# Attention's small products two pairs of heads at a time, in five spots of a layer in place of six

## The chip, the cores and the metric

One core of a Trainium2 chip runs the whole program. The metric is the device time of one launch in microseconds (us). The engines are TensorE (PE, matrix products; PEld is its loading of the stationary operand), VectorE (DVE, elementwise work and reductions), ScalarE (ACT, activations and copies), GpSimd (POOL) and SyncE (SP, which issues the transfers). PSUM is the memory that TensorE writes; it has eight banks of 128 partitions by 512 float32.

## The reference

A trunk of two layers on 256 positions of 1024 channels in float32. Each layer is a SwiGLU feed-forward block, a mixer, and a second feed-forward block. The mixer runs two branches on the same normalised input:

```python
h = rms_norm(x, mix_norm)
z = h @ w_in                      # 512 u, 512 q, 512 k, 512 v, 2048 gate logits
y_pool = multiscale_pool(u, pool_w, pool_scale)    # 4 groups of 128 channels:
                                  # (mean over the last 2/4/8/16 positions - token) @ pool_w[g]
q = rope(rms_norm(q.reshape(B, S, N_HEADS, HEAD_DIM), q_norm))   # 8 heads of 64
k = rope(rms_norm(k.reshape(B, S, N_HEADS, HEAD_DIM), k_norm))
y_attn = moba_attention(q, k, v)  # one block of 256 positions: plain causal attention
gates = jax.nn.sigmoid(gl + b_gate).reshape(B, S, N_BRANCH, D)
merged = gates[:, :, 0] * (y_pool @ w_branch_pool) + gates[:, :, 1] * (y_attn @ w_branch_attn)
x = x + merged @ w_out
```

With 256 positions and blocks of 256, no block is fully past, so attention is causal attention inside the one block.

## The kernel before, in words

**Weights.** Each weight arrives as a *unit*, a 1 MB tile `raw` of 128 by 2048 float32. `unit()` issues its transfer and splits it: ScalarE rounds each half to `hi` (line 111), VectorE takes the rest `lo` = `raw` - `hi` (line 112). A product by a weight is then a chain of two TensorE instructions per block (`chain`): `hi` against both parts of the activation at once (512 columns), `lo` against the first part (256 columns). There are six halves each of `hi` and `lo`, three units in all, so splitting runs ahead of TensorE until the buffers are full and then waits for TensorE to finish with the oldest half.

**Order.** TensorE's products stand in the order of the program (`keep`, line 76). The instructions of ScalarE and VectorE are put in a fixed order when the kernel is built: among those that the builder's own clock holds ready, the one that stands first in the program. On the chip each engine then runs its list in order and waits at whatever is not ready.

**PSUM.** The pool `pmm` has two buffers of two banks. The pool `pat` has the other four banks: two buffers of two banks inside the mixer (`half_psum(2)`), four of one bank elsewhere.

**The gates.** `gate(f)`, f from 0 to 7, multiplies one unit by the normalised input (`pair`: 16 chains, 32 instructions) into one `pmm` buffer and empties it with `drain`: ScalarE copies one part to `gates[:, f]` (line 157), VectorE adds the other (line 158). `open_gate(f)` then multiplies by the norm's factor (line 482) and applies tanh (line 485). As `pmm` has two buffers, gate f + 2 writes the buffer that the drain of gate f must have left.

**Attention.** The eight heads go as four pairs p. For each pair there are four steps: `scores(p)`, products with 64 rows of contraction, one head in each half of the rows; `softmax` (VectorE: mask, line 416, two maxima, line 421, reciprocal, line 428, scaling, line 431; ScalarE: four exponentials, line 426); `by_key(p)`, six transposes (line 438), copied to SBUF by ScalarE (`to_key`, line 442); `values(p)`, products with 64 columns of stationary operand, one head in each half of the columns; and `heads_end(p)`, which splits the result for the next product. These small products are plain float32, and so are the four products of the pooling branch, `pool_map(g)`, emptied by `map_end(g)`. `pool_diff`, VectorE work of the pooling branch, precedes them.

The small products stand between the gates' chains. Of a layer's six spots, the first is in the middle of gate 0 (`first`: scores 0, softmax 0, `pool_diff`), four are calls of `between(p)` behind gates 1, 3, 5 and 7, and the last is among the products of the branches (`branch`), which follow the gates:

| spot | small products in their order |
|---|---|
| middle of gate 0 | scores 0 |
| behind gate 1 | scores 1, by_key 0 |
| behind gate 3 | values 0, scores 2, by_key 1, map 0 |
| behind gate 5 | values 1, scores 3, by_key 2, map 1 |
| behind gate 7 | values 2, by_key 3, maps 2 and 3 |
| among the branches | values 3 |

Of the kernel before, what the change touches and what calls it, by code (L numbers as in the profile page):

```python
# [18 lines left out]
F32 = mybir.dt.float32  # L19
F32R = mybir.dt.float32r  # L20
AF = mybir.ActivationFunctionType
# [4 lines left out]
P = 128  # L26
# [3 lines left out]
NK = D // P  # L30
DFF = 2816
NF = DFF // P
NH = 8
DH = 64
GW = 512
# [13 lines left out]
def trunk_kernel(ctx: ExitStack, tc: tile.TileContext, x_in, w_in, pw_in, qkn_in, rope_in, mask_in, band_in, out):  # L49
# [5 lines left out]
    acts = ctx.enter_context(tc.tile_pool(name="acts", bufs=1))  # L55
# [5 lines left out]
    def quarter(name):  # L61
        return pat.tile([P, 2, S], F32, name=name, tag="at")
# [6 lines left out]
    pat = None  # L69
# [3 lines left out]
    act = nc.scalar.activation  # L73
# [4 lines left out]
    def mm(*args, **kw):  # L78
        return keep(nc.tensor.matmul(*args, **kw))  # L79

    def banks(pool, name):

        return pool.tile([P, 2, 2, S], F32, name=name, tag="mm" if pool is pmm else "at2")
# [6 lines left out]
    def unit():  # L90

        if ahead:
            return ahead.pop(0)
        raw, hi, lo = buffers()
        u = n_unit[0]
        n_unit[0] += 1
        n = HALF if u < 4 else 2 * HALF
        for c in range(0, 2 * HALF, n):
            nc.sync.dma_start(raw[:, c:c + n], w_in[u, :, c:c + n])
        for h in range(2):  # L100
            split(raw[:, h * HALF:(h + 1) * HALF], hi[h], lo[h])
        return hi, lo
# [44 lines left out]
    def pair(w, t, other=None, at=0):  # L147

        ps = banks(pmm, "ps")
        columns(w, ps, range(at))  # L150
        if other:
            other()
        columns(w, ps, range(at, NK))
        drain(t, ps)
# [46 lines left out]
    for t in range(PAD - 1):  # L201
        g = min(g for g, w in enumerate(WINDOWS) if t < w - 1)
# [145 lines left out]
    def tokens():  # L348

        pt = pmm.tile([P, 2, GW], F32, name="pt", tag="mm")  # L350
        for kh in range(2):
            hi, lo = unit()
            for t in range(2):
                ts = slice(t * P, (t + 1) * P)
                for kk in range(4):
                    k = kh * 4 + kk
                    wh, wl = blk(hi, 4 * kk, 4), blk(lo, 4 * kk, 4)
                    prod(pt[:, t], hx[:, k, 0, ts], wh, k == 0, False)
                    prod(pt[:, t, :S], hx[:, k, 0, ts], wl[:, :S], False, False)
                    prod(pt[:, t], hx[:, k, 1, ts], wh, False, False)  # L360
                    prod(pt[:, t, S:], hx[:, k, 0, ts], wl[:, S:], False, k == NK - 1)
        return pt

    def normed(pt, rt, name):
        z = acts.tile([P, 2, GW], F32, name=name, **({"tag": "v"} if name == "v" else {"tag": "tok", "bufs": 2}))
        for t in range(2):
            act(z[:, t, :], pt[:, t], AF.Copy, scale=rt[:, t:t + 1])
        return z
# [30 lines left out]
        for t in range(2):  # L399
            act(zT[:, :, t * P:(t + 1) * P], tp[:, t], AF.Copy)  # L400

    def scores(qT, kT, p):

        sc = banks(pat, "sc").rearrange("p h a s -> p h (a s)")
        for c, qs, ks in ((slice(0, S), slice(P, S), slice(0, S)), (slice(S, 3 * P), slice(0, P), slice(0, P))):
            for h in range(2):
                hs = slice(h * DH, (h + 1) * DH)
                mm(sc[:, h, c], lhsT=qT[hs, p, qs], rhs=kT[hs, p, ks], start=True, stop=True)  # L410
        return sc

    def softmax(sc):

        dg = sc[:, :, P:3 * P].rearrange("p h (a b) -> p h a b", a=2)
        tt(dg, dg, mask.unsqueeze(1).unsqueeze(1).to_broadcast([P, 2, 2, P]), op=OP.add)
        nb = small.tile([P, 2, 2], F32, name="nb", tag="nb")
        su = small.tile([P, 2, 2], F32, name="su", tag="su")
        cols = (slice(0, S), slice(S, 3 * P))
        for j, c in enumerate(cols):  # L420
            nc.vector.tensor_reduce(nb[:, j, :], sc[:, :, c], axis=AX.X, op=OP.max)
        nc.vector.tensor_scalar(nb, nb, -(DH ** -0.5), None, op0=OP.mult)
        pr = acts.tile([P, 2, GW], F32, name="pr", tag="tok", bufs=2)
        for h in range(2):
            for j, c in enumerate(cols):
                act(pr[:, h, c], sc[:, h, c], AF.Exp, scale=DH ** -0.5, bias=nb[:, j, h:h + 1],
                    accum_out=su[:, j, h:h + 1])
        nc.vector.reciprocal(su, su)
        for j, c in enumerate(cols):
            n = c.stop - c.start  # L430
            tt(pr[:, :, c], pr[:, :, c], su[:, j, :].unsqueeze(2).to_broadcast([P, 2, n]), op=OP.mult)  # L431
        return pr

    def by_key(pr, pt):

        for h in range(2):
            for o, c in enumerate((2, 0, 1)):
                keep(nc.tensor.transpose(pt[:, h, o * P:(o + 1) * P], pr[:, h, c * P:(c + 1) * P], ident))  # L438

    def to_key(pt):  # L440
        pT = acts.tile([P, 2, GW], F32, name="pT", tag="tok", bufs=2)
        act(pT[:, :, :3 * P], pt[:, :, :3 * P], AF.Copy)
        return pT

    def values(pT, v, p, y):

        for i, t in ((0, 0), (1, 0), (1, 1)):
            for s in range(2):
                h = 2 * p + s
                c = (i + t) * P  # L450
                mm(y[s * DH:(s + 1) * DH, i], lhsT=v[:, t, h * DH:(h + 1) * DH],
                   rhs=pT[:, s, c:c + P], start=t == 0, stop=t == i)

    def by_half(z):
        return z.rearrange("p (i c) -> p i c", c=P)

    def mix(l, after):
        pt = tokens()
# [3 lines left out]
        pt = tokens()  # L462
# [4 lines left out]
        qk = acts.tile([P, 12, S], F32, name="qk", tag="gb")  # L467
        qT, kT, pw = qk[:, :4, :], qk[:, 4:8, :], qk[:, 8:10, :].rearrange("p a (b c) -> p (a b) c", c=P)
        nc.sync.dma_start(pw, pw_in[l])
        gates = acts.tile([P, NK, 2, S], F32, name="gates", tag="gates")  # L470
# [7 lines left out]
        def gate(f, *other):  # L478
            pair(unit(), gates[:, f], *other)

        def open_gate(f):
            tt(gates[:, f], gates[:, f], bc2(r), op=OP.mult)
            for j in range(2):
                c = j * NK + f
                act(gates[:, f, j, :], gates[:, f, j, :], AF.Tanh, scale=0.5, bias=hb[:, c:c + 1])
# [37 lines left out]
        def pool_map(g, yp):  # L523

            for i in range(2):
                mm(yp[:, i], lhsT=pw[:, g, :], rhs=uT[:, g, PAD + i * P:PAD + (i + 1) * P], start=True, stop=True)

        def map_end(g, yp):
            sc = hb[:, C_PS - C_BG + g:C_PS - C_BG + g + 1]
            hi, lo = by_half(pk[g][:, 0, :]), by_half(pk[g][:, 1, :])  # L530
            act(hi, yp, AF.Copy, scale=sc)
            stt(lo, yp, sc, hi.bitcast(F32), op0=OP.mult, op1=OP.subtract)

        norm_rope(q, qkn[:, l, 0])
        v = normed(tokens(), rh, "v")
# [1 line left out]
        to_features(q, qT)  # L537
        project_u()
        to_features(k, kT)
        NP = NH // 2  # L540

        def heads_end(p, y):

            act(by_half(yk[p][:, 0, :]), y, AF.Copy)
            tt(by_half(yk[p][:, 1, :]), y, by_half(yk[p][:, 0, :]).bitcast(F32), op=OP.subtract)

        def between(p):

            nonlocal pr, pT
            pt = banks(pat, "pt").rearrange("p h a s -> p h (a s)")  # L550
            rest = slice(3 * P, 4 * P)
            if p:
                values(pT, v, p - 1, pt[:, :, rest])
            if p + 1 < NP:
                sc = scores(qT, kT, p + 1)
            by_key(pr, pt)
            maps = []
            if p + 1 == NP:
                yp = banks(pat, "yp")
                maps = [(p - 1 + i, by_half(yp[:, i, 0])) for i in range(2)]  # L560
            elif p:
                maps = [(p - 1, sc[:, :, rest])]
            for z in maps:
                pool_map(*z)
            pT = to_key(pt)
            if p + 1 < NP:
                pr = softmax(sc)
            if p:
                heads_end(p - 1, pt[:, :, rest])
            for z in maps:  # L570
                map_end(*z)

        pT = pr = None

        def first():
            nonlocal pr
            pr = softmax(scores(qT, kT, 0))
            pool_diff()

        for h in range(NH):  # L580
            gate(h, *((first, NK // 2) if h == 0 else ()))
            if h % 2:
                between(h // 2)
            open_gate(h)

        def branch(f, j, k0=0, k1=4):
# [16 lines left out]
        for f in (0, 1, 3, 2):  # L603
            for j in range(2):
                branch(f, j, 0, 2)
        y = quarter("y")[:, :, :P]
        values(pT, v, NP - 1, y)
        heads_end(NP - 1, y)
        for f in range(4):
            branch(f, 0, 2)  # L610
        for f in range(4):
# [26 lines left out]
    for f in range(0, NK, 2):  # L638
        c = L * NG + (f + 2) * S
# [114 lines left out]
```

## Time and profile before

| what | us |
|---|---|
| median of three runs | 1012.44 |
| the three runs | 1017.16, 1012.44, 1007.99 |
| span of the profiled execution, first to last instruction | 1006.2 |

The profile gives the profiled execution's span and no other time of its own. The shortest of the three runs is 1.8 us above that span, the median 6.2 us. Times in the rows are us from the start of the span. A row of the timeline has start, duration, engine, line, operation, tile written and tiles read, shapes, the count of merged instructions and, in brackets, the idle time before it and what ended that. Matmuls are pipelined: one starts while the one before still drains, so what an instruction costs TensorE is the distance from its start to the next one's start, not its duration. The same holds in part for VectorE and ScalarE, whose neighbouring instructions overlap by about 0.1 us.

### The profile page before, as it was taken

Reading aid. Unit: us, or ns where it says so; the run is one execution under the profiler, and the core shown is the slowest. Engines: PE = TensorE matmul, PEld = TensorE weight load, DVE = VectorE, ACT = ScalarE, POOL = GpSimd, SP = SyncE. Lnnn points to the kernel's source line nnn. Section 1 sums busy time; section 2 is a strip of 40 time slices with the busy share of each in tenths; the row PEclk is TensorE's granted clock in tenths of the full one; section 3 lists DMA queues with packets and bytes.
Section 4 is the critical chain, followed back from the end, with each engine's and each line's share of the span. In section 5 each row is a group of like instructions: output and inputs, shape, how many; then the busy total and the mean of one; then the engine's idle time right before and its main releaser. Section 6 shows DMA issues by size and latency. Waiting matters only on the chain.

```text
span 1006.2 us, 16021 instructions
## 1 busy us (share of the span) xinstructions
PE 1000.7 (99%) x6348; PEld 906.3 (90%) x6348; DVE 795.7 (79%) x1193; ACT 625.4 (62%) x983; POOL 1.4 (0%) x26
## 2 busy tenths in 40 slices
PE   9999999999999999999999999999999999999998
PEld 8899989898899999999999998998988998999898
DVE  7998866699779788886678888666998798888752
ACT  7866655567756766665576666556676567665641
POOL 0000000000000000000000000000000000000000
PEclk9999999999999999999999999999999999999999
DMA  8765555644527565555556655655544375646640
GB/s 302 277 239 205 185 202 201 220 151 172 181 85 251 174 214 205 204 190 203 196 172 209 210 202 188 203 196 194 191 168 145 110 256 173 231 178 209 209 147 22
DMA packets 29882, 192.89 MB, mean 192 GB/s; under 512 B 3312, under 2 KB 4592, under 8 KB 7280
## 3 DMA queue, kind: packets, MB, share of 16 engines
q1 hardware_dynamic: 29808, 191.88, 55.1%
q8 instruction: 49, 0.80, 0.3%
q14 instruction: 25, 0.20, 0.1%
HBM read 190.82 MB, written 1.05 MB: 191 GB/s over the span
## 4 chain that ended last, share of the span: by engine, by line
PE 92%; DVE 5%; ACT 1%; issue 1%; DMA 0%; SPq 0%
PE ps L79 79%; PE pt L79 7%; PE two L79 4%; DVE lo L112 2%; ACT hi L111 1%; PE sc L79 1%; PE pe L79 0%; DMA raw<-w 0%; PE pt L438 0%; DVE gates L513 0%; DVE ab L321 0%; DVE uT L520 0%; DVE gates L158 0%; DVE gates L509 0%; DVE pr L431 0%
## 5 line engine op out<-in xcount | busy, mean ns | idle before, releaser
L79 PE MATMUL ps<-hx,hi 128*128 128x512 f32 x1712 | 574.4, 383 | 0.6 <-ACT hi L111 0.3
L112 DVE TENSOR_TENSOR lo<-raw,hi 128x1024 fp32r<-128x1024 f32 (+2 forms) x367 | 440.2, 1203 | 128.9 <-ACT hi L111 124.4
L111 ACT ACTIVATE hi<-raw 128x1024 fp32r<-128x1024 f32 (+2 forms) x367 | 378.7, 1039 | 217.3 <-PE ps L79 172.1
L79 PE MATMUL ps<-hx,lo 128*128 128x256 f32 x1712 | 468.6, 274 | 0.2 <-DVE lo L112 0.2
L79 PEld LDWEIGHTS ps<-hx,hi 128*128 128x128 f32 x1712 | 321.3, 188 | 58.3 <-DVE ab L158 0.8
L79 PEld LDWEIGHTS ps<-hx,lo 128*128 128x128 f32 x1712 | 322.0, 188 | 0.9 <-DVE lo L112 0.8
L79 PE MATMUL ps<-ga,hi 128*128 128x512 f32 (+1 forms) x528 | 172.4, 376 | 0.0
L79 PE MATMUL ps<-ga,lo 128*128 128x256 f32 x512 | 140.0, 273 | 0.0
L79 PEld LDWEIGHTS ps<-ga,hi 128*128 128x128 f32 x528 | 97.9, 188 | 16.5
L79 PEld LDWEIGHTS ps<-ga,lo 128*128 128x128 f32 x512 | 96.3, 188 | 0.0
L79 PE MATMUL ps<-gb,hi 128*128 128x512 f32 (+1 forms) x198 | 65.6, 376 | 0.0
L79 PE MATMUL pt<-hi,hx 128*128 128x512 f32 x192 | 65.1, 385 | 0.0
L321 DVE TENSOR_TENSOR ab<-ab,r 128x512 f32<-128x512 f32 x88 | 60.3, 691 | 2.4
L158 DVE TENSOR_TENSOR ab<-ps,ab 128x512 f32<-128x512 f32 x87 | 59.7, 688 | 2.2
L323 ACT ACTIVATE sg<-ab 128x256 f32<-128x256 f32 x88 | 36.7, 417 | 32.0 <-DVE ab L321 28.7
L79 PE MATMUL pt<-lo,hx 128*128 128x256 f32 x192 | 52.7, 274 | 0.0
L79 PE MATMUL ps<-gb,lo 128*128 128x256 f32 x192 | 52.5, 273 | 0.0
L157 ACT ACTIVATE ab<-ps 128x512 f32<-128x512 f32 x87 | 50.4, 580 | 0.5 <-PE ps L79 0.5
L174 ACT ACTIVATE ga<-sg 128x256 fp32r<-128x256 f32 x64 | 26.4, 417 | 35.4 <-DVE sg L324 34.3
L79 PE MATMUL two<-ax,hi 128*128 128x256 f32 x256 | 44.9, 278 | 0.3
L79 PE MATMUL ps<-ax,hi 128*128 128x256 f32 x256 | 44.1, 276 | 0.0
L79 PEld LDWEIGHTS ps<-gb,hi 128*128 128x128 f32 x198 | 36.7, 188 | 6.2
(148 smaller groups left out, 857.1 us busy)
## 6 DMA issues: line engine op xcount, KB each, us to landing
raw<-w SPq DMA_DIRECT2D x176, 1024.0 KB, 4.9
raw<-w SPq DMA_DIRECT2D x12, 256.0 KB, 5.7
raw<-w SPq DMA_DIRECT2D x2, 512.0 KB, 6.2
out_dram<-gx SPq DMA_DIRECT2D x8, 128.0 KB, 1.9
gx<-x SPq DMA_DIRECT2D x3, 256.0 KB, 6.0
qk<-pw SPq DMA_DIRECT2D x2, 256.0 KB, 2.7
gx<-x SPq DMA_DIRECT2D x1, 300.0 KB, 2.6
qkn<-qkn SPq DMA_DIRECT2D x1, 256.0 KB, 5.1
```

The costliest lines, as they stand in the source:

```text
L79: return keep(nc.tensor.matmul(*args, **kw))
L111: act(hi, w, AF.Copy)
L112: tt(lo, w, hi.bitcast(F32), op=OP.subtract)
L157: act(t, ps[:, :, 1, :], AF.Copy)
L158: tt(t, ps[:, :, 0, :], t, op=OP.add)
L174: act(d[:, 0, :], v, AF.Copy)
L321: tt(ab, ab, bc2(r[0]), op=OP.mult)
L323: act(sg, ab[:, 0, :], AF.Silu)
```

## The change

The four pairs of heads go two at a time. `first` computes the scores of pairs 0 and 1 in the middle of gate 0, followed in the program by both softmaxes and then `pool_diff`. `turn_two(0)` behind gate 2 transposes both, with pool maps 0 and 1. `middle`, in the middle of gate 4, computes values 0 and 1 and scores 2 and 3, with their softmaxes behind. `turn_two(2)` behind gate 6 transposes pairs 2 and 3, with maps 2 and 3. Values 2 and 3 are among the branches. The copies by key, two at a time now, lie in memory that is unused at that time: in `gates[4..7]` for pairs 0 and 1, in the memory of `qT` and `kT` for pairs 2 and 3.

| spot | small products in their order |
|---|---|
| middle of gate 0 | scores 0, scores 1 |
| behind gate 2 | by_key 0, by_key 1, maps 0 and 1 |
| middle of gate 4 | values 0, values 1, scores 2, scores 3 |
| behind gate 6 | by_key 2, by_key 3, maps 2 and 3 |
| among the branches | values 2, values 3 |

Nothing follows gate 7 but the branches. The products themselves, their shapes and their number are as before.

```diff
-    def scores(qT, kT, p):
-        sc = banks(pat, "sc").rearrange("p h a s -> p h (a s)")
+    def scores(qT, kT, p, sc):
         for c, qs, ks in (...):
...
-    def to_key(pt):
-        pT = acts.tile([P, 2, GW], F32, name="pT", tag="tok", bufs=2)
-        act(pT[:, :, :3 * P], pt[:, :, :3 * P], AF.Copy)
-        return pT
...
-        def between(p):
-            nonlocal pr, pT
-            pt = banks(pat, "pt").rearrange("p h a s -> p h (a s)")
-            rest = slice(3 * P, 4 * P)
-            if p:
-                values(pT, v, p - 1, pt[:, :, rest])
-            if p + 1 < NP:
-                sc = scores(qT, kT, p + 1)
-            by_key(pr, pt)
-            ...
-            pT = to_key(pt)
-            if p + 1 < NP:
-                pr = softmax(sc)
-            if p:
-                heads_end(p - 1, pt[:, :, rest])
-            for z in maps:
-                map_end(*z)
+        late = [gates[:, NH // 2:].rearrange("p f a s -> p (f a s)"), qk[:, :8].rearrange("p a s -> p (a s)")]
+        pTs = [z[:, i * 2 * GW:(i + 1) * 2 * GW].rearrange("p (h c) -> p h c", h=2) for z in late for i in range(2)]
+        rest = slice(3 * P, 4 * P)
+        prs = []
+        def flat(name):
+            return banks(pat, name).rearrange("p h a s -> p h (a s)")
+        def score_two(p, scs):
+            for i, sc in enumerate(scs):
+                scores(qT, kT, p + i, sc)
+            prs[:] = [softmax(sc) for sc in scs]
         def first():
-            pr = softmax(scores(qT, kT, 0))
+            score_two(0, [flat("sc") for _ in range(2)])
             pool_diff()
+        def turn_two(g):
+            pts = [flat("pt") for _ in range(2)]
+            for pr, pt in zip(prs, pts):
+                by_key(pr, pt)
+            for i, pt in enumerate(pts):
+                pool_map(g + i, pt[:, :, rest])
+            for pT, pt in zip(pTs[g:], pts):
+                act(pT[:, :, :3 * P], pt[:, :, :3 * P], AF.Copy)
+            for i, pt in enumerate(pts):
+                map_end(g + i, pt[:, :, rest])
+        def values_two(p, ys):
+            for i, y in enumerate(ys):
+                values(pTs[p + i], v, p + i, y)
+        def middle():
+            scs = [flat("sc") for _ in range(2)]
+            ys = [sc[:, :, rest] for sc in scs]
+            values_two(0, ys)
+            score_two(2, scs)
+            for p, y in enumerate(ys):
+                heads_end(p, y)
+        inside = {0: first, 4: middle}
         for h in range(NH):
-            gate(h, *((first, NK // 2) if h == 0 else ()))
-            if h % 2:
-                between(h // 2)
+            gate(h, *((inside[h], NK // 2) if h in inside else ()))
+            if h in (2, 6):
+                turn_two(h // 4 * 2)
             open_gate(h)
...
-        y = quarter("y")[:, :, :P]
-        values(pT, v, NP - 1, y)
-        heads_end(NP - 1, y)
+        ys = [quarter("y")[:, :, :P] for _ in range(2)]
+        values_two(2, ys)
+        for p, y in enumerate(ys):
+            heads_end(2 + p, y)
```

More of the change, by code (lines that the diff above doesn't have):

```diff
@@ L410, in scores @@
                 mm(sc[:, h, c], lhsT=qT[hs, p, qs], rhs=kT[hs, p, ks], start=True, stop=True)
-        return sc
     def softmax(sc):
@@ L539, in mix @@
         to_features(k, kT)
-        NP = NH // 2
         def heads_end(p, y):
@@ L545, in heads_end @@
             tt(by_half(yk[p][:, 1, :]), y, by_half(yk[p][:, 0, :]).bitcast(F32), op=OP.subtract)
-        def between(p):
-            nonlocal pr, pT
-            pt = banks(pat, "pt").rearrange("p h a s -> p h (a s)")
-            rest = slice(3 * P, 4 * P)
-            if p:
-                values(pT, v, p - 1, pt[:, :, rest])
-            if p + 1 < NP:
-                sc = scores(qT, kT, p + 1)
-            by_key(pr, pt)
[L557 to L562, printed above, removed]
-            for z in maps:
-                pool_map(*z)
-            pT = to_key(pt)
-            if p + 1 < NP:
-                pr = softmax(sc)
-            if p:
-                heads_end(p - 1, pt[:, :, rest])
-            for z in maps:
-                map_end(*z)
@@ L573, in mix @@
-        pT = pr = None
+        late = [gates[:, NH // 2:].rearrange("p f a s -> p (f a s)"), qk[:, :8].rearrange("p a s -> p (a s)")]
[8 more added lines that the diff above has]
+            prs[:] = [softmax(sc) for sc in scs]
@@ L575, in first @@
         def first():
-            nonlocal pr
-            pr = softmax(scores(qT, kT, 0))
+            score_two(0, [flat("sc") for _ in range(2)])
             pool_diff()
+        def turn_two(g):
[8 more added lines that the diff above has]
+                map_end(g + i, pt[:, :, rest])
```

## The prediction

> **What bounds the kernel now.** I read the page's engine shares and the chain first, then TensorE's row of the timeline through the attention stage of layer 0 (layer 1 repeats it), then VectorE and ScalarE where TensorE waits for them.
>
> ```profile
> PE 1000.7 (99%) x6348; PEld 906.3 (90%) x6348; DVE 795.7 (79%) x1193; ACT 625.4 (62%) x983; POOL 1.4 (0%) x26
> PE 92%; DVE 5%; ACT 1%; issue 1%; DMA 0%; SPq 0%
> 232.00:242.50 10.50, 10.44 (x70) 9.06 (x70) 10.38 (x24) 7.79 (x15) 0.00 (x0) 1.00 0.51 184
> ```
>
> The first two lines say TensorE: busy 99% of the span, 92% of the chain. The 5% of VectorE in the chain has a place, and the third line (a window around gates 0 and 1; the columns after the length are PE, PEld, DVE, ACT, POOL, clock, DMA share, GB/s) shows it: for 10.5 us VectorE is busy for 10.38. TensorE is not yet late there, but it has no slack either. So the change can help only by shortening what TensorE does or waits for, at most a few microseconds of a thousand, and it can hurt wherever it puts more in front of TensorE in the one stretch where VectorE is full.
>
> **What it removes on TensorE.** The products stay. What can go is the cost of passing between kinds of product. First an insertion of transposes between two chains, then the whole spot behind gate 3:
>
> ```profile
> 216.59 0.27 PE L79 MATMUL pt<-lo,hx 128*128 128x256 f32 x1
> 216.70 1.03 PE L398 MATMUL tp<-ident,q 128*128 128x128 f32 x8
> 217.49 0.47 PE L79 MATMUL ps<-hx,hi 128*128 128x512 f32 x1
> 217.80 0.28 PE L79 MATMUL ps<-hx,lo 128*128 128x256 f32 x1
> ...
> 253.28 0.27 PE L79 MATMUL ps<-hx,lo 128*128 128x256 f32 x1
> 253.49 0.88 PE L79 MATMUL pt<-pT,v 128*64 128x128 f32 x12
> 254.29 0.93 PE L79 MATMUL sc<-qk 64*128 64x256 f32 x8
> 255.15 0.88 PE L438 MATMUL pt<-ident,pr 128*128 128x128 f32 x6
> 255.86 0.61 PE L79 MATMUL sc<-uT,qk 128*128 128x128 f32 x4
> 256.22 0.48 PE L79 MATMUL ps<-hx,hi 128*128 128x512 f32 x1
> 256.54 0.28 PE L79 MATMUL ps<-hx,lo 128*128 128x256 f32 x1
> ```
>
> A `lo` product takes 0.11 us to the next start (216.59 to 216.70) and a `hi` product 0.22 in a steady chain; a gate's 16 chains therefore take 16 x 0.33 = 5.3 us. The eight transposes with the edges on both sides take 217.80 - 0.22 - 216.70 = 0.88, or 0.11 each: entering and leaving the spot costs nothing. All of these use the full 128 by 128 array. The second block has the same edges, and in addition values on 64 columns ("128*64") and scores on 64 rows ("64*128"). It takes 256.54 - 0.22 - (253.28 + 0.11) = 2.93 us. At 0.11 us per 128 columns its work is 6 units of values (12 instructions, two heads side by side), 6 of scores (8 instructions, two side by side, half of them 256 columns wide), 6 transposes and 4 instructions of the map: 22 x 0.11 = 2.42. The missing 0.51 us fall on three passages: full to columns, columns to rows, rows to full; 0.17 each.
>
> The passages count by kind, then, not by spot. Before, a layer has 2 + 2 + 3 + 3 + 2 + 2 = 14 of them (spots in order). After, the middle of gate 0 has 2, the spots behind gates 2 and 6 have none (transposes and maps are full array, as in the first block), the middle of gate 4 has 3, the branches 2: 7. The saving is 7 x 0.17 = **1.2 us a layer**. [...] By that rule the count is 7; were it the edges of the spots (12 before, 10 after), it would be 2 x 0.17 = 0.3 us. The first block, where edges cost nothing, bears the rule out.
>
> **The wait in front of gate 2.** This is where I expect the change to pay.
>
> ```profile
> 240.82 0.27 PE L79 MATMUL ps<-hx,lo 128*128 128x256 f32 x1
> 241.03 0.93 PE L79 MATMUL sc<-qk 64*128 64x256 f32 x8
> 242.01 0.85 PE L438 MATMUL pt<-ident,pr 128*128 128x128 f32 x6
> 242.62 0.49 PE L79 MATMUL ps<-hx,hi 128*128 128x512 f32 x1
> ```
> ```profile
> 236.30 1.23 DVE L112 TENSOR_TENSOR lo<-raw,hi 128x1024 fp32r<-128x1024 f32 x1
> 237.77 1.23 DVE L112 TENSOR_TENSOR lo<-raw,hi 128x1024 fp32r<-128x1024 f32 x1
> ...
> 241.87 0.69 DVE L158 TENSOR_TENSOR gates<-ps,gates 128x512 f32<-128x512 f32 x1
> 242.47 1.22 DVE L112 TENSOR_TENSOR lo<-raw,hi 128x1024 fp32r<-128x1024 f32 x1
> ```
>
> The first rows are the end of gate 1, the spot behind it, and the first product of gate 2 at 242.62. That product writes the `pmm` buffer of gate 0, whose drain (L158) begins on VectorE at 241.87 and has ended when the next operation starts, at 242.47. Gate 2 is released 0.15 us before it starts. The drain is that late because `pool_diff` and softmax 0 stand before it in the program and keep VectorE full (the window's row).
>
> After the change TensorE comes to gate 2 sooner: the transposes go behind gate 2, scores 1 go into gate 0 (6 x 0.11 = 0.66, no passage of their own). It arrives at 240.82 + 0.11 + 0.66 = 241.6. The drain of gate 0 comes later, since softmax 1 now also stands before it in the program. What that is:
>
> ```profile
> L416 DVE TENSOR_TENSOR sc<-sc,mask x8: 692/693/696, 234.0 to 769.3; 128x512 f32<-128x512 f32 x8
> L421 DVE TENSOR_REDUCE nb<-sc x16: 416/552/692, 235.0 to 770.8; 128x2 f32<-128x512 f32 x8, 128x2 f32<-128x256 f32 x8
> L431 DVE TENSOR_TENSOR pr<-pr,su x16: 419/554/693, 240.8 to 774.1; 128x512 f32<-128x512 f32 x8, 128x256 f32<-128x256 f32 x8
> 238.06 0.47 ACT L426 ACTIVATE pr<-sc,nb 128x256 f32<-128x256 f32 x1
> ...
> 239.66 0.61 ACT L157 ACTIVATE gates<-ps 128x512 f32<-128x512 f32 x1
> ```
>
> Durations in ns (least, median, most): one softmax is 0.69 + 2 x 0.55 + 2 x 0.55 and two tiny operations, 3.0 us; neighbours overlap by about 0.1 (L158 above, 0.69 long, is followed after 0.60), so 2.6 us of a full queue. ScalarE's four exponentials take 239.66 - 238.06 = 1.6. From both sides: with the order of before and softmax 1 inserted, the drain ends at 242.5 + 2.6 = 245.1, and TensorE waits 3.5 us. If softmax 1 fills the moments in which the two `lo` of 236.30 and 237.77 slipped in (1.1 each, the overlap off), it would be 242.9, but then ScalarE is late: its copy moves from 239.66 by 1.6 (exponentials 1) and 0.66 (later products) to 241.9, and with 0.61 and 0.69 behind it the drain ends at 243.2, a wait of 1.6. I take one `lo` displaced: mask and maxima of pair 1 are ready for the first gap, its scaling is not for the second. 244.0, a wait of **2.4 us** (1.6 to 3.5). Everything on TensorE queues behind it. The wait for `pr` in front of the transposes goes (241.03 to 242.01 is 0.98 where the same scores take 0.86 behind gate 3): **-0.1**. What is late next, gate 3 behind gate 1's drain, has 5.3 us more and is covered.
>
> **The wait behind gate 7.**
>
> ```profile
> 280.67 0.88 PE L79 MATMUL pt<-pT,v 128*64 128x128 f32 x12
> ...
> 283.00 0.47 PE L79 MATMUL two<-ax,hi 128*128 128x256 f32 x2
> ...
> 284.34 0.27 PE L79 MATMUL two<-ax,lo 128*128 128x256 f32 x1
> 284.74 0.50 PE L79 MATMUL two<-ax,hi 128*128 128x256 f32 x2
> ```
> ```profile
> 284.00 0.68 DVE L158 TENSOR_TENSOR gates<-ps,gates 128x512 f32<-128x512 f32 x1
> ```
> ```profile
> 103.69 1.06 ACT L111 ACTIVATE hi<-raw 128x1024 fp32r<-128x1024 f32 x1 [1.03 <-PE ps L79]
> 105.92 0.68 DVE L158 TENSOR_TENSOR ab<-ps,ab 128x512 f32<-128x512 f32 x1
> ```
>
> The second pair of `two` takes gate 7's buffer. Its drain ends at 284.68; TensorE, done with the first 12 branch products (283.00 to 284.45), waits 0.3 us. Gate 7 ended about 280.6 (the next product starts at 280.67), so the drain took 4.1 us, and the spot behind gate 7 hid 2.4 of them. That cover goes; 1.45 us are left. With the same 4.1 the wait is 2.65. But the softmax that delayed this drain has moved to gate 4, so I take a drain of the feed-forward block (the last two rows), from ScalarE's release by TensorE at 103.69 to 106.60: 2.9, a wait of 1.45. With nothing queued it is 0.6 + 0.7, and no wait. Net of 0.3: **+1.15** (-0.3 to +2.35).
>
> **Edits that cost nothing.** Softmaxes 2 and 3 in gate 4: VectorE has 2 x 2.6, `heads_end` 0.8, the drain 0.6 and up to two `lo`, 6.6 to 8.9 us; gate 6 needs that drain 0.66 + 2.67 + 5.33 = 8.7 us after scores 2. Taken at 0, up to 0.4. The transposes behind gates 2 and 6 come 13 us after their scores. The copies in `gates[4..7]` are read before gate 4 drains. No transfer moves on SP's queue, and POOL has nothing here.
>
> **Sum.** Per layer -1.2 - 0.1 + 2.4 + 1.15 = +2.25; two layers **+4.5**. The profiled execution (span 1006.2) becomes 1010.7. The median of the runs, 6.2 above that span, becomes **1017**.
>
> **The rivals.**
> - *The covers hold* (0.27). The builder's order puts gate 0's drain ahead of softmax 1's tail, and gate 7's drain meets empty queues. For: VectorE is only 79% busy overall. Against: the program's order, which the drain at 241.87 follows. Then only -1.2, -0.1 and -0.3 remain, -3.2 for both layers: 1009.
> - *The clock falls in the wait* (0.08), the slower side. If TensorE stands idle long enough for its clock to halve, the wait costs more than itself. This row is the start of the span:
>
> ```profile
> 1.05 4.21 PE L79 MATMUL busy<-ones 128*128 128x128 f32 x18 [1.05 <-DVE eps L190]
> ```
>
>   18 products in 4.21 us are 0.23 each, where such a product later takes 0.11. A spell as long would lose 2.1 us. With the upper waits (3.5 and 2.65, so +4.85 a layer) it is 2 x (4.85 + 2.1) = +14: 1026. [...]
> - *It doesn't save what it should* (0.10): passages cost by spot, 0.3 instead of 1.2 a layer, and the waits come: +6.3, 1019.
> - The forecast has 0.55, its own range 1012 to 1022 (waits of 1.6 and 0, or 3.5, 2.65 and 0.4).
>
> **How the numbers follow.** The three runs lie 9 us apart, so 1% (10 us) is about what a measurement of this kernel can tell from no change. Faster by over 1% needs 1002, beyond the best case: 0.02. Slower, over 1022.6: the clock's case and the forecast's top, 0.12. Within 1%: 0.86. The range, 1007 to 1023, takes in the first rival with some scatter of the runs and leaves out the clock and the far ends.
>
> **What would show it.** Right: a wait of TensorE of some 2 us at the first product of gate 2 and of some 1.5 us at the second pair of `two`, both released by L158; spots behind gates 2 and 6 at 0.11 us per instruction without edges; the middle of gate 4 at about 0.5 us over its 24 units of work. Wrong: L158 of gate 0 ahead of softmax 1's L431 in VectorE's order, no wait at gate 2, or a granted clock under 1.00 between 240 and 250 us.

## The result, and the profile after

| | us |
|---|---|
| changed kernel, median of 6 runs | 1017.39 (1015.8 to 1021.24) |
| kernel before, median of 6 runs | 1010.0 (1007.99 to 1017.16) |
| ratio after / before | 1.0075, 95% interval 1.0052 to 1.0098 |
| span of the profiled execution | 1014.0 (before 1006.2) |

The change costs 0.7%, inside the 1% that the prediction called no change. The time forecast was 1017.0. Three further runs of the kernel before brought its median from 1012.44 to 1010.0, though, so the measured difference is 7.4 us, not the 4.5 forecast. What follows is about differences.

The page's engine shares and chain, after:

```profile
PE 1000.9 (99%) x6348; PEld 907.0 (89%) x6348; DVE 797.0 (79%) x1193; ACT 625.7 (62%) x983; POOL 1.4 (0%) x26
PE 91%; DVE 5%; DMA 1%; ACT 1%; issue 1%; SPq 0%; DVEq 0%; ACTq 0%
```

They hardly differ from before. A change of this size isn't read from shares. The windows of the two mixers, from the first transposes to the end of the branches, show where it lies: first before (layers 0 and 1), then after. Columns: from:to, length, then busy time of PE, PEld, DVE, ACT and POOL, granted clock (the share of its full speed that TensorE was given), DMA share, GB/s.

```profile
216.70:306.50 89.80, 89.61 (x651) 81.52 (x650) 75.70 (x130) 59.20 (x111) 0.00 (x0) 1.00 0.45 157
714.30:804.10 89.80, 89.61 (x651) 81.51 (x650) 75.02 (x125) 59.19 (x111) 0.00 (x0) 1.00 0.44 157
```
```profile
218.20:310.60 92.40, 88.63 (x650) 81.48 (x649) 76.19 (x129) 59.20 (x111) 0.00 (x0) 1.00 0.43 153
718.00:812.10 94.10, 90.33 (x650) 82.82 (x649) 75.59 (x124) 59.07 (x111) 0.00 (x0) 0.98 0.43 150
```

Layer 0's mixer is 2.6 us longer and layer 1's 4.3. Two more things show. In layer 0 TensorE is busy 1.0 us *less* (89.61 to 88.63) in a stretch 2.6 us longer: something was saved, and more was waited. And layer 1 has a granted clock of 0.98. The rest of the 7.8 us between the spans is 1.5 ahead of the first mixer (216.70 to 218.20), where the programs don't differ, and -0.6 between and behind the mixers. The first mixer's start varies from run to run: in the profiled executions below it lies between 216.5 us (experiment 8) and 225.6 (experiment 5), and the program in front of it is the same in all of them. So a single time says little, and the windows of the mixers say more.

TensorE's longest waits after, by releaser (us in total, times, longest); before, no wait in the middle of the span was over 0.3:

```profile
PE ps L79 <- DVE gates L158: 4.4, 2, 2.2
PE two L79 <- DVE gates L158: 3.2, 2, 1.6
```

**Gate 2.** TensorE's and VectorE's timeline in layer 0, around the first product of gate 2:

```profile
242.99 0.27 PE L79 MATMUL ps<-hx,lo 128*128 128x256 f32 x1
245.44 0.49 PE L79 MATMUL ps<-hx,hi 128*128 128x512 f32 x1 [2.18 <-DVE gates L158]
```
```profile
239.76 1.22 DVE L112 TENSOR_TENSOR lo<-raw,hi 128x1024 fp32r<-128x1024 f32 x1
243.42 1.02 DVE L427 TENSOR_TENSOR pr<-pr,su 128x512 f32<-128x512 f32 x2
244.36 0.42 DVE L511 SCALAR_TENSOR_TENSOR uT<-gates,uT 128x256 f32<-128x256 f32 x1
244.69 0.69 DVE L158 TENSOR_TENSOR gates<-ps,gates 128x512 f32<-128x512 f32 x1
```

Gate 1's last product takes 0.11 us, and the next starts 2.45 us after it: a wait of 2.34 us. (The bracket counts from the modelled end, 0.16 later.) It ends with gate 0's drain, L158 at 244.69, which stands behind softmax 1's scaling (L427) and `pool_diff` (L511).

**The spots.** TensorE behind gate 2, and in the middle of gate 4:

```profile
250.88 1.47 PE L434 MATMUL pt<-ident,pr 128*128 128x128 f32 x12
252.18 1.06 PE L79 MATMUL pt<-uT,qk 128*128 128x128 f32 x8
253.00 0.47 PE L79 MATMUL ps<-hx,hi 128*128 128x512 f32 x1
253.30 0.27 PE L79 MATMUL ps<-hx,lo 128*128 128x256 f32 x1
...
260.97 0.27 PE L79 MATMUL ps<-hx,lo 128*128 128x256 f32 x1
261.18 1.53 PE L79 MATMUL sc<-gates,v 128*64 128x128 f32 x24
262.64 1.58 PE L79 MATMUL sc<-qk 64*128 64x256 f32 x16
264.14 0.49 PE L79 MATMUL ps<-hx,hi 128*128 128x512 f32 x1
264.47 0.28 PE L79 MATMUL ps<-hx,lo 128*128 128x256 f32 x1
```

By the prediction's way of counting, the full-array spot takes 253.30 - 0.22 - 250.88 = 2.20 us for 20 instructions, 0.11 each, with no edges. The middle of gate 4 takes 264.47 - 0.22 - (260.97 + 0.11) = 3.17 for 24 units of 0.11 (2.64), so 0.53 for its three passages.

**The branches.** Gate 7 has ended about 285.13. TensorE at the second pair of `two`; ScalarE; VectorE:

```profile
286.39 0.27 PE L79 MATMUL two<-ax,lo 128*128 128x256 f32 x1
288.25 0.49 PE L79 MATMUL two<-ax,hi 128*128 128x256 f32 x2 [1.59 <-DVE gates L158]
```
```profile
285.28 1.06 ACT L111 ACTIVATE hi<-raw 128x1024 fp32r<-128x1024 f32 x1 [1.58 <-PE ps L79]
286.24 0.58 ACT L157 ACTIVATE gates<-ps 128x512 f32<-128x512 f32 x1
```
```profile
286.37 1.23 DVE L112 TENSOR_TENSOR lo<-raw,hi 128x1024 fp32r<-128x1024 f32 x1 [1.41 <-ACT hi L111]
287.51 0.68 DVE L158 TENSOR_TENSOR gates<-ps,gates 128x512 f32<-128x512 f32 x1
```

The wait is 288.25 - 286.39 - 0.11 = 1.75 us. Gate 7's end also frees the half that the next `hi` is written to, so ScalarE splits first (1.06) and copies second; on VectorE the `lo` stands in front of L158 in the same way. A drain of 0.6 + 0.7 takes 3.1 us (285.13 to 288.25).

**The clock.** Behind the same wait in layer 1 (TensorE's timeline, then the windows behind gate 2's first product in layer 1 and in layer 0):

```profile
746.03 0.63 PE L79 MATMUL ps<-hx,hi 128*128 128x512 f32 x1
746.46 0.42 PE L79 MATMUL ps<-hx,lo 128*128 128x256 f32 x1
```
```profile
745.30:749.60 4.30, 4.30 (x16) 3.71 (x17) 4.30 (x6) 2.08 (x4) 0.00 (x0) 0.60 0.51 152
245.50:251.00 5.50, 5.50 (x34) 4.96 (x35) 5.50 (x7) 4.07 (x7) 0.00 (x0) 1.00 0.56 191
```

A `hi` product takes 0.43 us there (746.03 to 746.46) in place of 0.22. The trace's clock record has one spell at half speed in the mixers, 3.41 us long (0.50 from 745.95 to 749.36), so 1.7 us lost: exactly what layer 1 lost more than layer 0 (94.10 - 92.40). Layer 0 has the same wait and a granted clock of 1.00.

### The profile page after: what moved, and what is told of

Same layout as the page of the kernel before. It is cut to its first block, busy times and chain, and to the rows that moved or that the text cites. A ratio compares the mean times of both kernels' runs of the same rounds, so it can differ in the third digit from the quotient of the medians.

```text
span 1014.0 us, 16012 instructions
## 1 busy us (share of the span) xinstructions
PE 1000.9 (99%) x6348; PEld 907.0 (89%) x6348; DVE 797.0 (79%) x1193; ACT 625.7 (62%) x983; POOL 1.4 (0%) x26
## 4 chain that ended last, share of the span: by engine, by line
PE 91%; DVE 5%; DMA 1%; ACT 1%; issue 1%; SPq 0%; DVEq 0%; ACTq 0%
PE ps L79 79%; PE pt L79 7%; PE two L79 4%; DMA raw<-w 1%; DVE lo L112 1%; ACT hi L111 1%; PE sc L79 1%; PE pt L434 1%; DVE gates L504 0%; DVE nb L417 0%; DVE pr L427 0%; DVE ab L321 0%; PE y L79 0%; DVE uT L511 0%; DVE gates L158 0%
## 5 line engine op out<-in xcount | busy, mean ns | idle before, releaser
L158 DVE TENSOR_TENSOR ab<-ps,ab 128x512 f32<-128x512 f32 x87 | 59.8, 688 | 2.3
```

The costliest lines, as they stand in the source:

```text
L158: tt(t, ps[:, :, 0, :], t, op=OP.add)
```

## The experiments

Theory: the seven passages saved are worth about 1 us a layer; two new waits, each for a drain that the change put later or uncovered, cost more; half-clock spells follow some of them. Rivals: the waits are symptoms and the time goes elsewhere; passages don't count by kind; the spells come by chance. Every edit is against the changed kernel, and no kernel leaves work out.

The first four were compared with 29 runs of the kernel before on their chip, median 1009.16.

**1. Gate 0's drain first.** Softmax 1 and `pool_diff` go behind gate 0 in the program; TensorE's order stays.

```diff
...
-            score_two(0, [flat("sc") for _ in range(2)])
-            pool_diff()
+            scs = [flat("sc") for _ in range(2)]
+            for p, sc in enumerate(scs):
+                scores(qT, kT, p, sc)
+            prs[:] = [softmax(scs[0])]
+            held.append(scs[1])
...
+            if h == 0:
+                prs.append(softmax(held[0]))
+                pool_diff()
```

> The changed kernel, with softmax 1 and pool_diff placed behind gate 0's drain in the program (the products stay where they are). Theory (the wait in front of gate 2 is a matter of order: gate 0's drain stands behind softmax 1 and pool_diff on VectorE and behind its exponentials on ScalarE): the wait of 2.34 us in each layer falls to 0.0 to 0.4, and with it the spell of half clock that follows it in layer 1 (1.7 us); the wait at the second pair of two stays at 1.75. Time: the changed kernel's 1017.4 less 2 x 2.1 and less 1.7, about 1011.5, 0 to 0.3% over the kernel before. Rival (VectorE has too much to do between gates 0 and 2, in whatever order): about 2 us stay at gate 2 or come back at gate 3 or at the transposes, and the time stays at 1016 to 1017.

Measured: 1010.72 (12 runs), ratio 1.0021 (1.0004 to 1.0039). TensorE's waits, then VectorE's timeline:

```profile
PE ps L79 <- DVE gates L158: 0.3, 2, 0.2
PE two L79 <- DVE gates L158: 3.2, 2, 1.6
```
```profile
243.16 0.68 DVE L158 TENSOR_TENSOR gates<-ps,gates 128x512 f32<-128x512 f32 x1
244.26 1.02 DVE L427 TENSOR_TENSOR pr<-pr,su 128x512 f32<-128x512 f32 x2
```

The drain now stands ahead of softmax 1's scaling. That is less than the program's order says: the builder keeps softmax 1's mask and maxima, and most of `pool_diff`, ahead of the drain on VectorE; what has moved behind it is the scaling and three of `pool_diff`'s four operations of L511. Gate 2's wait has all but gone, the branches' wait is untouched, and the granted clock is 0.999 or 1.000 in all 12 runs. The excess of 7.4 us falls to 1.6.

**2. The cover back behind gate 7.** The last transposes and maps move from gate 6 to gate 7.

```diff
-            if h in (2, 6):
+            if h in (2, 7):
```

> The changed kernel, with the second pair of transposes and maps behind gate 7 in place of gate 6. Theory (the wait at the second pair of two is gate 7's drain, 3.1 us from the end of the gate to its release, without the cover that stood behind gate 7): 2.1 us of small products and 1.45 of the branches cover it, the wait of 1.75 us a layer goes to 0, the wait in front of gate 2 stays at 2.3, and the time is about 1017.4 - 3.5 = 1013.9, 0.3 to 0.5% over the kernel before. Rival (the drain is late because the engines are behind, and gets later with the copies): a wait of 1 us or more stays, at the same place or in front of values 2, and the time stays over 1016.

Measured: 1011.71 (12 runs), ratio 1.0017 (1.0001 to 1.0032). TensorE's waits:

```profile
PE ps L79 <- DVE gates L158: 4.4, 2, 2.2
```

The wait at `two` has gone from the list, gate 2's is as it was. The mechanism is as expected; the time is 2 us better than expected. One cause is in the records: the granted clock is 0.998, that of one spell (1.7 us of 1010), in only 6 of the 12 runs and 1.000 in the other six, while every run of the changed kernel has 0.996 to 0.998.

**3. Both.**

> Both edits together: softmax 1 and pool_diff behind gate 0's drain, the second transposes behind gate 7. Theory: both waits go, the saving of seven passages (1.04 us a layer in the trace) and of the two short waits of the kernel before (0.13 and 0.29) is left: 2 x 1.2 = 2.4 us under the kernel before, ratio 0.996 to 0.999. Rival (the saving is taken back by another wait that the two hid, or the passages did not cost what the trace says): no faster than before, ratio 1.000 or more.

Measured: 1007.58 (12 runs), ratio 0.9981 (0.9963 to 0.9999), granted clock 0.999 or 1.000 throughout. The wait list and the two mixers:

```profile
PE ps L79 <- DVE gates L158: 0.3, 2, 0.2
```
```profile
216.70:305.30 88.60, 88.43 (x650) 81.48 (x649) 76.06 (x129) 58.98 (x111) 0.00 (x0) 1.00 0.45 160
712.70:801.30 88.60, 88.43 (x651) 81.46 (x649) 75.37 (x124) 58.94 (x111) 0.00 (x0) 1.00 0.45 159
```

With both waits out, each mixer is 1.2 us shorter than before (89.80 to 88.60), so 2.4 us in all; the medians differ by 1.6. This is the change's gain once nothing takes it back, and it is the best version here, ahead of both kernels by a little.

**4. Two more passages in the middle of gate 4.** The same 40 instructions, pair by pair.

```diff
-            values_two(0, ys)
-            score_two(2, scs)
+            for i in range(2):
+                values(pTs[i], v, i, ys[i])
+                scores(qT, kT, 2 + i, scs[i])
+            prs[:] = [softmax(sc) for sc in scs]
```

> The changed kernel, with the middle of gate 4 in the order values 0, scores 2, values 1, scores 3: the same 40 instructions in the same spot with five passages between kinds of product in place of three. Theory (passages cost, 0.17 us each): the spot takes 2.97 + 2 x 0.17 = 3.3 us from its first start to the next gate product. Rival (what costs is entering and leaving a spot): it stays at 2.97.

Measured, one run: 1019.13. Its time can't tell 0.7 us; TensorE's timeline in layer 0 can:

```profile
263.19 0.88 PE L79 MATMUL sc<-gates,v 128*64 128x128 f32 x12
263.99 0.92 PE L79 MATMUL sc<-qk 64*128 64x256 f32 x8
264.85 0.88 PE L79 MATMUL sc<-gates,v 128*64 128x128 f32 x12
265.65 0.92 PE L79 MATMUL sc<-qk 64*128 64x256 f32 x8
266.51 0.49 PE L79 MATMUL ps<-hx,hi 128*128 128x512 f32 x1
```

266.51 - 263.19 = 3.32 us, where the changed kernel has 264.14 - 261.18 = 2.96: 0.36 for two passages more inside one spot. They count by kind, at 0.18 each.

The next four were meant to settle what brings the half clock. They share 9 runs of the kernel before, median 1008.51.

**5. A longer wait, by a longer `pool_diff`** (its first sum made twice).

```diff
-                    tt(dst[:, :, lo:], src[:, 1:, lo:], src[:, 1:, lo - h:W - h], op=OP.add)
+                    for _ in range(2 if i == 0 else 1):
+                        tt(dst[:, :, lo:], src[:, 1:, lo:], src[:, 1:, lo - h:W - h], op=OP.add)
```

> The changed kernel, with the first and largest operation of pool_diff done twice (the second time writes the same values again), 1.03 us more on VectorE in front of gate 0's drain. Theory (the half clock follows from the length of TensorE's wait): the wait in front of gate 2 becomes 3.2 to 3.5 us in both layers, and a spell of 3.41 us of half clock follows in each of them, mean granted clock 0.997 or less in every run; the time is 2.0 us above the changed kernel's for the waits and up to 1.7 more for spells that it did not have in every run, 1019 to 1021. Rival (the spells come by chance, whatever the wait): as often as in the changed kernel, a mixture of 1.000, 0.998 and 0.997.

Measured: 1014.61 (6 runs), ratio 1.0056 (1.0042 to 1.0069). A miss: the wait became shorter. TensorE's waits, and VectorE:

```profile
PE ps L79 <- DVE gates L158: 3.3, 2, 1.6
```
```profile
251.50 0.68 DVE L158 TENSOR_TENSOR gates<-ps,gates 128x512 f32<-128x512 f32 x1
252.10 1.42 DVE L512 SCALAR_TENSOR_TENSOR uT<-gates,uT 128x256 f32<-128x256 f32 x4
```

The builder takes what its own clock holds ready. With `pool_diff` later by one operation, its four weighted differences (L512 here, L511 in the changed kernel) all went behind the drain; in the changed kernel all four stand ahead of it. As an accident it is of use: at waits of 1.8 us (the list's 1.6, and 0.16) no run of six shows a spell (granted clock 0.999 or 1.000), and the kernel is 2.9 us faster than the changed one beside it although VectorE does more. The run with the profile is its slowest, 1020.81 at full clock; it is the one whose first mixer starts at 225.6 us.

**6. The changed kernel again, beside it.**

> The changed kernel once more, for its time and clock beside the others on one chip. Expected 0.5 to 1.0% over the kernel before; mean granted clock by run 0.996 to 1.000, since waits of 2.34 us were followed by a spell in one layer of the profiled execution and not in the other.

Measured: 1017.51 (5 runs), ratio 1.0091 (1.0077 to 1.0104). Granted clock 0.997 in all five, and the windows behind gate 2's first product in both layers:

```profile
243.80:248.50 4.70, 4.65 (x17) 3.96 (x18) 4.70 (x7) 2.29 (x5) 0.00 (x0) 0.64 0.53 174
745.50:750.00 4.50, 4.47 (x17) 3.85 (x18) 4.50 (x7) 2.20 (x4) 0.00 (x0) 0.62 0.51 160
```

The same program has two spells here and one in the first profile; its wait in layer 0 is 2.33 us here and 2.34 there.

**7 and 8. One half of the first experiment each:** `pool_diff` alone behind gate 0's drain, then softmax 1 alone.

```diff
             score_two(0, [flat("sc") for _ in range(2)])
-            pool_diff()
...
+            if h == 0:
+                pool_diff()
```
```diff
-            score_two(0, [flat("sc") for _ in range(2)])
+            ... (scores 0 and 1, softmax 0)
             pool_diff()
...
+            if h == 0:
+                prs.append(softmax(held[0]))
```

> The changed kernel, with pool_diff alone behind gate 0's drain in the program; softmax 1 stays ahead of it. Theory (softmax 1 ahead of the drain is the larger part; the operations of pool_diff are ready early and fill gaps wherever they stand): the wait in front of gate 2 only falls from 2.34 to about 1.9. Rival (pool_diff is what makes VectorE full): it falls under 0.5.

> The changed kernel, with softmax 1 alone behind gate 0's drain in the program; pool_diff stays ahead of it. Theory: ScalarE's copy of the drain comes before the exponentials of pair 1 and VectorE's part before the scaling of pair 1; what stays is the last three operations of pool_diff, 0.34 us each, ahead of it: the wait falls from 2.34 to 1.0 to 1.4. Rival (softmax 1 is not the cause): it stays over 2.

Measured, one run each: 1017.39 and 1010.42. Gate 2's wait with `pool_diff` moved, then with softmax 1 moved:

```profile
PE ps L79 <- DVE gates L158: 3.7, 2, 1.8
```
```profile
PE ps L79 <- DVE gates L158: 2.0, 2, 1.0
```

By the starts of the products the waits are 2.0 and 1.15 us: of the 2.0 us between 2.34 and experiment 1's 0.3, softmax 1 alone takes out 1.2 and `pool_diff` alone 0.3; together they take out more than the sum of these two. On VectorE experiment 7 moved one operation only, the last of the four L511 (0.41 us). The rest of `pool_diff` still stands ahead of the drain, so this run doesn't settle the rival in which `pool_diff` is what makes VectorE full. Layer 1 of the first has a spell behind a wait of 2.00 us (a `hi` product takes 0.43 us from 748.01 on). Layer 0 has none behind 2.0: the whole run's granted clock is 0.998, that of one spell. The second has none (1.000).

**9. A wait of about four us, without moving anything in the program.** ScalarE's copy in gate 0's drain is written five times, with the same values. (Compared with 7 runs of before, median 1008.61.)

```diff
...
-    def drain(t, ps):
-        act(t, ps[:, :, 1, :], AF.Copy)
+    def drain(t, ps, times=1):
+        for _ in range(times):
+            act(t, ps[:, :, 1, :], AF.Copy)
...
-            pair(unit(), gates[:, f], *other)
+            pair(unit(), gates[:, f], *other, times=5 if f == 0 else 1)
```

> The changed kernel with one difference: ScalarE's copy in the drain of gate 0 (L158 reads what it wrote; 0.63 us each) is written five times, each time the same values, so that the drain of gate 0 comes about 1.8 to 2.5 us later and nothing else changes its place in the program. Theory (a spell of half clock of 3.41 us follows when 2.0 us or more of a wait fall into one stretch of a fixed 3.41 us grid): the wait in front of gate 2 becomes about 4 us (3.6 to 4.8), and as a wait of 4.0 us puts at least 2.0 us into one stretch wherever it lies, a spell follows in both layers in every run: granted clock of the whole run 0.997 or less in each, a stretch of some 3.4 us at about half clock behind gate 2's first product in both layers; time: the two waits longer by 1.7 to 2.0 each over the changed kernel with two spells (1017.5), so about 1021, 1.2 to 1.3% over before. Rival (spells come by chance, or from something else than the wait): some runs at 0.998 to 1.000, and the time spread over 3.4 us. Second rival (the builder's order moves again, as it did when pool_diff was lengthened): the wait is not longer than 2.4 us, and the run says nothing of the grid.

Measured: 1020.84 (4 runs), ratio 1.012 (1.0057 to 1.0183); granted clock 0.995, 0.994, 0.997 and 0.996. Waits (the drain's addition is line 159 in this kernel), the first product of gate 2 in layer 0, and the windows behind gate 2's first product in layer 0 and in layer 1:

```profile
PE ps L79 <- DVE gates L159: 6.8, 2, 3.4
243.22 0.27 PE L79 MATMUL ps<-hx,lo 128*128 128x256 f32 x1
246.90 0.80 PE L79 MATMUL ps<-hx,hi 128*128 128x512 f32 x1 [3.41 <-DVE gates L159]
```
```profile
246.90:252.10 5.20, 5.20 (x16) 4.42 (x17) 4.25 (x5) 2.84 (x6) 0.00 (x0) 0.50 0.81 244
750.80:754.00 3.20, 3.20 (x10) 2.71 (x11) 3.15 (x4) 2.83 (x6) 0.00 (x0) 0.50 0.85 300
```

The wait is 3.57 us, just under the 3.6 to 4.8 expected. Split evenly, that would be 1.79 us in each of two stretches, so the argument of the expectation doesn't bind every run. In the profiled execution the stretch of 3.41 us ahead of the spell holds 2.2 us of the wait in layer 0 and 3.4 in layer 1, by where the half clock begins. Every run's mean clock is that of two spells or more (0.997 and less), so chance alone is out. (VectorE's list did move a little: one `lo` split now stands ahead of the drain.) One thing wasn't foreseen: layer 0's spell lasts 6.8 us, twice the 3.41 of layer 1 in the changed kernel. By the granted clock of two more windows, 0.90 from 240.00 to 246.90 and 0.61 from 246.90 to 253.90, it is half for 1.4 us ahead of gate 2's first product and for 5.5 us behind.

## Why the prediction was right, and where its sizes were off

- **The passages.** Forecast -1.2 a layer. What is left of layer 0's +2.6 once the waits below are taken out is 2.6 - 2.34 - 1.46 + 0.13 = -1.1; experiment 3, which has neither wait, gives -1.2 a mixer with everything in it. Spots behind gates 2 and 6 without edges, 0.53 in the middle of gate 4, and 0.36 for two added passages (experiment 4) bear out the count by kind. The rival by which they cost by spot (0.10) is out.
- **The wait for `pr`** ahead of the transposes: forecast -0.1, measured -0.13.
- **Gate 2.** Forecast 2.4 (1.6 to 3.5), measured 2.34. The reading chosen, one `lo` displaced and one still ahead of the drain, is what VectorE's rows show (`lo` at 239.76, the drain behind L427). Experiment 1 takes the wait away by moving softmax 1's scaling, which the prediction named, and part of `pool_diff`; softmax 1 alone is worth 1.2 of it (experiment 8). The rival that the covers hold (0.27) is out: both drains came late. How much of the 2.34 is `pool_diff`'s stays open (experiment 7).
- **The branches.** Forecast 1.45, measured 1.75. The term mis-sized is the drain's length, 2.9 forecast from the feed-forward block and 3.1 here; the other 0.1 is the branch products in front of the wait, 1.45 forecast and 1.37 here (285.13 to 286.50). The net +1.15 is +1.46. Experiment 2 shows that a cover behind gate 7 is enough to take the wait away.
- **Taken at nothing.** Gate 6 has no wait; the term of 0 stands.
- **The clock.** This is the step that failed. The prediction made it a rival of 0.08, put at the upper waits (3.5 and 2.65 us), with a price of 2.1 us in each layer. Its price was near (1.7, for 3.41 us at half clock), its waits too long: behind waits of 2.0 to 2.34 us a spell came in some layers, and such waits lay in the forecast itself. The trace of before, with no wait over 0.3 in its middle, couldn't show that. The spells therefore belonged in the sum, with +1.7 in one or both layers, rather than at its far end. The prediction's own sign of being wrong, a granted clock under 1.00 between 240 and 250 us, is absent from the first profile of the changed kernel, and experiment 6 has it (0.64 from 243.80 to 248.50). That rival's sum also holds a slip: its +4.85 a layer counts the branches' wait of 2.65 without taking off the 0.3 of before. With 4.55 the time is 1025.7, so the 1026 stands.

With the measured terms, two layers cost 2 x 2.6 = 5.2, and one or two spells 1.7 or 3.4: 6.9 to 8.6 us, with 7.4 measured. The forecast of 4.5 is short by 0.4 a layer (0.3 of it the branches' wait, the rest the passages) and by the spells. That the time itself was met to 0.4 us is partly luck: it was put on a median of before that later runs lowered by 2.4 us. What stays open is why the profiled execution of after begins its first mixer 1.5 us later; experiment 6, the same kernel, reaches gate 2's first product in layer 0 about 1.6 us earlier than the first profile did, so it varies by run, and no run shows why.

## What to carry to other kernels

Grouping small products by the shape of the array they use paid here by the number of passages saved: 0.17 us each in the spot behind gate 3 of the kernel before, 0.18 inside the middle of gate 4. But each insertion between two large products is also a cover for a drain, and the work issued with it stands ahead of another drain: when spots move, name for each accumulator who empties it, what now stands in front of that on its engine, and what TensorE did meanwhile. Put the drain that the next large product needs ahead of the work that nobody waits for; here that and one moved spot turned 0.7% of loss into 0.2% of gain.

## What the runs showed of the hardware that was not expected

Behind some TensorE waits of 2.0 to 3.6 us the granted clock was half for 3.4 us or more, and behind others it stayed full, with waits of 2.34 us on both sides. The waits are counted by the products' starts. The clock is that of the window named; where none is named, it is the mean of the profiled execution.

| kernel, layer | wait, us | granted clock | spell behind the wait |
|---|---|---|---|
| after, 0 | 2.34 | 1.00 (245.50 to 251.00) | no |
| after, 1 | 2.34 | 0.50 (745.95 to 749.36) | yes, 3.41 us |
| experiment 2, 0 | 2.34 | 1.00 (240.00 to 251.00) | no |
| experiment 2, 1 | 2.34 | 0.84 (740.00 to 751.00) | yes |
| experiment 4, 0 and 1 | 2.34 | 0.998 | one, by the mean |
| experiment 6, 0 | 2.33 | 0.64 (243.80 to 248.50) | yes |
| experiment 6, 1 | 2.3 | 0.62 (745.50 to 750.00) | yes |
| experiment 7, 0 | 2.0 | 0.998, which layer 1's spell accounts for | no |
| experiment 7, 1 | 2.00 | 0.998; `hi` products of 0.43 us from 748.01 | yes |
| experiment 9, 0 | 3.57 | 0.50 (246.90 to 252.10) | yes, 6.8 us |
| experiment 9, 1 | 3.57 | 0.50 (750.80 to 754.00) | yes |
| experiments 1, 3, 5, 8 | 1.8 or less | 0.999 or 1.000 in every run | no |

The clock records of the first two profiles show a regularity. In after the clock is recorded full from 5.26 us of the span, half from 745.95 to 749.36, and half again from 1015.60, behind the last instruction. In before it is full from 5.59 and half from 1005.69. From full to half that is 740.69, 1010.35 and 1000.11 us, or 217, 296 and 293 times 3.4133 us, to within 2 ns. The author's reading is a grid of such stretches in each run. In after, layer 0's wait (243.10 to 245.44) is then split at 244.19, which is 70 stretches on, into 1.09 and 1.25 us and has no spell; layer 1's (742.88 to 745.22) lies whole in the stretch from 742.54 to 745.95 and has one. Experiment 7's rows in layer 1 turn slow at about 747.6, so its 2.00 us lie in one stretch too.

In these cases, then, 2.00 us or more of one stretch came ahead of a spell and 1.25 did not. That was the reading before experiment 9, which was made to try it and fits with 2.2 and 3.4. Where in a stretch the waits of experiments 2, 4 and 6 and of layer 0 of experiment 7 lie is not shown here, so these rows neither bear the reading out nor speak against it. The ends of the first two traces fit it. TensorE's last product in before ends at 1002.94 and leaves 2.75 us of its stretch idle, and the next stretch is at half clock (0.50 from 1005.70). In after it ends at 1010.77 and leaves 1.4, and the half clock begins a whole idle stretch later.

The first 1.4 us of experiment 9's longer spell are still the wait. In layer 1 of that run at most 0.05 us of the spell are, and in layer 1 of after and of experiment 7 none. No run was made to try whether that is why it lasts twice as long. Nor does any run show why the changed kernel has one spell in some executions and two in others. An estimate from the starts is that the same wait meets the grid elsewhere: in layer 0 gate 2's first product starts at 245.44 us in the first profile, with no spell, and at 243.85 in experiment 6, with one.
